# Gated linear attention on one core: gate ranks transposed with the keys a tile ahead, half of a compact score copy on another engine, weight splits tied to another instruction

## The chip, the core and the metric

The kernel runs on one NeuronCore of a Trainium2 chip. The metric is the device time of one execution in microseconds; the profile is one execution taken by the hardware profiler on the same core. The engines are TensorE (PE: matrix products and transposes; PEld is its load of the stationary operand), ScalarE (ACT: activations and copies), VectorE (DVE), GpSimd (POOL) and SyncE (SP), which here only issues DMAs. Products land in PSUM, in eight banks; everything else lies in SBUF.

## The reference

One step of a decoder layer for 2048 prompt tokens and 64 sample tokens, all float32. What matters here is group B of the mixer, gated linear attention with 4 heads (key width 64, value width 128):

```python
h = rms_norm(x, g_mix_pre)
proj = jnp.einsum('btd,de->bte', h, w_in)      # ... gq, gk, gv, gr and the 16 gate ranks glr
log_a = jax.nn.log_sigmoid(einsum('btr,rk->btk', glr, w_gk2) + b_gk) / GLA_GATE_TEMP
b = jnp.cumsum(log_a, in a chunk)              # decay of the keys
k_rel = jnp.exp(where(causal, b_t - b_s, -inf)) * k_s
o_intra = einsum(einsum(q, k_rel), v)          # inside a chunk
o_inter = (q * exp(b)) @ S                     # from the state
S = exp(b_last) * S + (k * exp(b_last - b)).T @ v
o = rms_norm(o, g_gla) * silu(gr)
```

Around it stand the combined input projection, sliding-window attention (group A), the output projection with norms and residual, and a squared-ReLU MLP of width 4096.

## The kernel before

The work is in tiles of 128 tokens: 16 of the prompt (`NB`) and one of the sample (number `NB`). The stages follow each other on the chip: projection and attention of group A (to about 345 us), the gated linear attention with its own projections (to about 745 us), the output projection, and the MLP, whose weights and activations are multiplied by a scheme of seven products on split operands. Float32 operands are split into a high and a low part and multiplied three times (`hi*hi`, `hi*lo`, `lo*hi`).

**The order of the work.** TensorE's order is the order of the code (the helper `te`, class `InOrder` at line 120, chains every product to the one before it). For ScalarE, VectorE, GpSimd and SyncE in this stage there is no such chain: a planner sorts their instructions at compile time, by the order of the code and by its own estimate of when each is ready, and may issue a later tile's step before an earlier tile's. `tc.issue_after(ins)` ties what a block adds on the engine of `ins` to come after `ins`.

**The gated linear attention.** `gla(i)` (line 1067) is a generator for tile i. It yields numbers: at each `yield n`, the driver (lines 1346 to 1356) takes n products from `fill` and puts them on TensorE; half way it advances `side`, the steps of the sample tile, once. `fill` (`products`, line 1293) are the projections of later tiles (tile name `gproj`, 24 products of 128x384 for each of four chunks of weights), then, when the last tile is projected, the first output projections (`out`), whose weights `wo` are loaded into the place of the chunks that are done. `G_FILL` (line 65) holds the five fills of a tile.

In a tile, in the order of the code:
- `qk_T` (964) turns queries and keys (`gqk`, bank d); VectorE copies the keys to `kt`, ScalarE the queries to `qz`.
- After the first fill (34), `finish_out` of the tile before ends: `ogT`, the transposed output.
- `decays` of the next tile (933), up to line 940: for an even tile the gate ranks of two tiles are turned (`pg`, bank d) and copied by ScalarE to `glrT`. Then the second fill (6).
- `put_diagonal` (1023): the diagonal of the scores into the compact tile `AH`.
- `level_sums` and `weighted` for seven levels (block sizes 1 to 64): running sums of the logs in `before` and `after`, their exponentials in `dec`, and keys and queries weighted with them, `XK` and `XQ`. Each level needs the one before it, in turn on VectorE (1014, 1015) and ScalarE (1011, 1013).
- `keys_decayed` (995): the keys decayed to the end of the tile, `kdT`.
- The rest of `decays` of the next tile: `z`, two products with `glrT`, then three ScalarE steps (945 to 947) and one VectorE step (948) that gives the next tile's `before`.
- `gate` (950), the swish gate `sg`. Then the third fill (24).
- `kdT` turned (bank e) and copied by ScalarE to `kd`. Then the fourth fill (8).
- The scores by level: `gl` and `gh` (bank c, 1101 to 1109), and `ds` (bank d), what the tile adds to the state.
- VectorE places the scores with masks in `AH` (1021, six levels). ScalarE copies the largest level from `gh` (1122) and then the two halves of `AH` (1124, 64 partitions x 256 each) to `AT`. VectorE makes the new state `S` (1127). Then the fifth fill (20).
- `o` (bank e): for each head the query part with the old state and `AT` with the values.
- A step of `split_wo` (1256): one of eight raw tiles of the output weights is split into a high part (ScalarE, 218) and a low part (VectorE, 219), stored to DRAM, and a further raw tile is loaded. The block stands under `tc.issue_after(done.ins)`, `done` being the second state update on VectorE.

`before`, `after`, `dec`, `sg`, `qz`, `AH` and `AT` have one place each, `kt`, `kd` and `zt` two. Banks d and e have one place, the other kinds (a, b, c) two. The sample tile goes through the same helpers from `gla_sample` (1153), with bank b.

Of the kernel before, what the change touches and what calls it, by code (L numbers as in the profile page):

```python
# [15 lines left out]
AF = mybir.ActivationFunctionType  # L16
# [5 lines left out]
P = 128  # L22
# [3 lines left out]
NB = T // P  # L26
# [35 lines left out]
G_FIRST = (0, 1)  # L62
G_NEXT = (NB, *range(2, NB))
G_ORDER = (0, 1, 2, 3)
G_FILL = (34, 6, 24, 8, 20)
S_WAIT = (3, 6)
WO_PARTS = ((), (0, 1, 2), (3, 4, 5), (6, 7))
B_ORDER = (*(j + b for j in range(4) for b in (0, 4)), NB, *(j + b for j in range(4) for b in (8, 12)))
# [47 lines left out]
def f32(ap):  # L116
    return ap.bitcast(F32)
# [23 lines left out]
def hybrid_step_kernel(ctx: ExitStack, tc: tile.TileContext, I, O):  # L141
    nc = tc.nc
# [20 lines left out]
    te, ac, dv = (InOrder(tc, engine) for engine in (nc.tensor, nc.scalar, nc.vector))  # L163
# [4 lines left out]
    def bank(shape, kind, name):  # L168

        return ps.tile(shape, F32, tag=kind, name=name, bufs=1 if kind in "de" else 2)  # L170
# [21 lines left out]
    ident = cpool.tile([P, P], F32, name="ident")  # L192
# [77 lines left out]
    glr = gp_pool.tile([P, (NTILE + 1) // 2, 2, HD], F32R, name="glr")  # L270
# [133 lines left out]
    half_of = slice(HD), slice(HD, P)  # L404
# [479 lines left out]
    def places(name, shape, n=1, kind=F32):  # L884
        return cycle([sp.tile(shape, kind, name=f"{name}{u}") for u in range(n)])

    S = [sp.tile([P, 2, P], F32, name=f"S{u}") for u in range(2)]
    glrT = [sp.tile([P, P], F32R, name=f"glrT{u}") for u in range(3)]
    AT = sp.tile([P, 4, P], F32, name="AT")
    AH = sp.tile([P, 4, HD], F32, name="AH")  # L890
# [10 lines left out]
    zts, kdTs = places("zt", [P, 2, P], 2), places("kdT", [P, 2, P])  # L901
# [28 lines left out]
    for t in (s_xk, s_qz, s_at, s_after):  # L930
        nc.gpsimd.memset(t, 0.0)

    def decays(i, n, before, kind="d"):

        gt = glrT[i // 2 % 2 if i < NB else 2]
        if i % 2 == 0:
            pg = bank([P, P], kind, f"pg_{i}")
            te.transpose(pg, f32(glr[:, i // 2]).rearrange("p a r -> p (a r)"), ident)
            nc.scalar.activation(gt, pg, AF.Copy)
        yield  # L940
        z = bank([P, 2, n], kind, f"z_{i}")
        for g in range(2):
            te.matmul(z[:, g], wgk[:, i % 2, g * P : (g + 1) * P], gt[:, :n], start=True, stop=True)
        t = next(zts)[:, :, :n]
        nc.scalar.activation(t, z, AF.Abs)
        nc.scalar.activation(t, t, AF.Exp, scale=-1.0)
        nc.scalar.activation(t, t, AF.Ln, bias=1.0)
        nc.vector.scalar_tensor_tensor(before, z, 0.0, t, op0=ALU.min, op1=ALU.subtract)
# [15 lines left out]
    def qk_T(i, gp, n, kind="d"):  # L964

        pt = bank([P, 2, 2, n], kind, f"gqk_{i}")
        for g in range(2):
            for a in range(2):
                src = gp[:n, (1 - a) * 256 + g * P : (1 - a) * 256 + (g + 1) * P]
                te.transpose(pt[:, g, a, :], src, ident[:n, :n])  # L970
        kt, q = (next(kts), qz) if n == P else (s_kt, s_qz)
        nc.vector.tensor_copy(kt, pt[:, :, 0, :])
        for r, rr in enumerate(half_of):
            nc.scalar.activation(q[rr, r], pt[rr, :, 1, :], AF.Copy, scale=0.125)
        return kt
# [16 lines left out]
        out = xq[:, l].rearrange("p r g (m b) -> p r (g m) b", b=b)  # L992
        nc.vector.tensor_tensor(out, dr.unsqueeze(1).to_broadcast(list(out.shape)), pairs(q, b, 1), op=ALU.mult)

    def keys_decayed(after, kt, kdT, n, kind, kd):

        nc.scalar.activation(kdT, after, AF.Exp, scale=1.0 / 16)
        nc.vector.tensor_tensor(kdT, kdT, kt, op=ALU.mult)
        yield
        pk = bank([P, 2, P], kind, f"kdT_{n}")  # L1000
        for g in range(2):
            te.transpose(pk[:n, g, :], kdT[:, g, :], ident)
        nc.scalar.activation(kd[:n], pk[:n].rearrange("p g k -> p (g k)"), AF.Copy)

    def level_sums(before, after, dec, l, b):

# [10 lines left out]
    def put_level(at, gm, mk, b):  # L1017

        dst = halves(at, b)[1]
        m = mk.rearrange("p (m b) -> p m b", b=b).unsqueeze(1).to_broadcast(list(dst.shape))  # L1020
        nc.vector.copy_predicated(dst, m, gm.rearrange("p h (m b) -> p h m b", b=b))

    def put_diagonal(i, at, gp, n):

        pr = next(prs)
        nc.vector.scalar_tensor_tensor(pr[:n], gp[:n, 0:256], 0.125, gp[:n, 256:512], op0=ALU.mult, op1=ALU.mult)
        dg = sp.tile([P, 4], F32, tag="dg", name=f"dg_{i}", bufs=2)
        nc.vector.tensor_reduce(dg[:n], pr[:n].rearrange("p (h d) -> p h d", h=4), op=ALU.add, axis=AX.X)
        shape = [n, 4, HD]
        nc.vector.copy_predicated(at, dmsk[:n].unsqueeze(1).to_broadcast(shape), dg[:n].unsqueeze(2).to_broadcast(shape))  # L1030
# [29 lines left out]
    def decayed(i):  # L1060

        before, after = next(befores), next(afters)
        yield from decays(i, P, before)
        nc.gpsimd.memset(after, 0.0)
        pre[i] = before, after

    def gla(i, gp, og=iter(())):

        assert {(i, 0), (i, 1)} <= projected
        before, after = pre.pop(i)
        next(og, None)
        kt = qk_T(i, gp, P)
        dec = next(decs)
        following = decayed(i + 1) if i < NB - 1 else iter(())
        yield G_FILL[0] if i else 24, True
        deque(og, 0)
        next(following, None)
        yield G_FILL[1], True  # L1080
        put_diagonal(i, AH, gp, P)
        for l, b in enumerate(LEVELS):
            level_sums(before, after, dec, l, b)
            if l == NL - 1:
                kd = next(kds)
                turned = keys_decayed(after, kt, next(kdTs), P, "e", kd)
                nc.scalar.activation(dec[:, NL], before, AF.Exp, scale=1.0 / 16)
            weighted(XK, XQ, dec, kt, qz, l, b)
        next(turned)
        deque(following, 0)  # L1090
        assert {(i, c) for c in range(4)} <= projected
        sg = gate(i, gp, P)
        yield G_FILL[2], True
        deque(turned, 0)
        yield G_FILL[3], True
        low = bank([P, 4, 4, P // 4], "c", f"gl_{i}")
        high = bank([P, 512], "c", f"gh_{i}")
        mid = high[:, :256].rearrange("p (l h q) -> p l h q", l=2, h=4)
        far = high[:, 256:384].rearrange("p (r q) -> p r q", r=2)
        levels = [*(low[:, l] for l in range(4)), *(mid[:, l] for l in range(2))]  # L1100
        for l, gm in enumerate(levels):
            for g in range(2):
                keys = XK[:, l, g] if l else kt[:, g]
                for u, uu in enumerate(half_of):
                    te.matmul(
                        gm[uu, 2 * g : 2 * g + 2], keys[:, uu], XQ[:, l, :, g, u * 32 : u * 32 + 32], start=True, stop=True
                    )
        for g in range(2):
            te.matmul(far[half_of[g]], XK[:, NL - 1, g, :HD], XQ[:, NL - 1, :, g], start=True, stop=True)
        gv = gp[:, 512:1024]  # L1110
        ds = bank([P, 2, P], "d", f"ds_{i}")
        for h in range(4):
            te.matmul(
                ds[half_of[h % 2], h // 2], kd[:, h * HD : (h + 1) * HD], gv[:, h * P : (h + 1) * P],
                start=True, stop=True,
            )
        qd = next(qds)
        nc.vector.tensor_tensor(qd, qz, dec[:, NL].unsqueeze(1).to_broadcast([P, 2, 2, P]), op=ALU.mult)
        for l, gm in enumerate(levels):
            put_level(AH, gm, msk[:, l], LEVELS[l])  # L1120
        for g in range(2):
            nc.scalar.activation(AT[:HD, 2 * g : 2 * g + 2, HD:], far[half_of[g]], AF.Copy)
        for uu in half_of:
            nc.scalar.activation(AT[uu, :, uu], AH[uu], AF.Copy)
        So, Sn = S[i % 2], S[(i + 1) % 2]
        for g in range(2):
            done = nc.vector.scalar_tensor_tensor(
                Sn[:, g], So[:, g], dec[:, NL, g, P - 1 : P], ds[:, g], op0=ALU.mult, op1=ALU.add
            )
        yield G_FILL[4], True  # L1130
        o_ = bank([P, 4, P], "e", f"o_{i}")
        for h in range(4):
            if i > 0:
                te.matmul(o_[:, h, :], qd[:, h % 2, h // 2], So[:, h // 2], start=True, stop=False)
            te.matmul(o_[:, h, :], AT[:, h, :], gv[:, h * P : (h + 1) * P], start=i == 0, stop=True)
        with tc.issue_after(done.ins):
            next(wo_parts, None)
        ogs_of[i] = og = finish_out(i, lambda h: o_[:, h, :], sg, P, "e")
        if i == NB - 1:
            yield from og  # L1140
            for g in range(2):
                for r in range(2):
                    nc.sync.dma_start(O["gla_prompt"][0, 0, 2 * g + r], Sn[half_of[r], g])
# [944 lines left out]
```

## Time and profile before

| what | value |
|---|---|
| median of 3 runs | 2264.04 us (2259.86 to 2265.18) |
| the profiled execution | 2263.19 us, span 2261.4 us |
| instructions | 34140 |
| granted TensorE clock, mean | 0.995 of full speed |
| TensorE / VectorE / ScalarE / GpSimd busy | 97 / 68 / 54 / 11% |
| gated linear attention | about 345 to 745 us |

How to read the profile: L12 is line 12 of the kernel; `out<-in` are the program's names of the tiles written and read; a row of the waits says who waited for whom, with the total in us, how often, and the longest; a row of a timeline gives start, duration, engine, line and operation, and in brackets the idle time of the engine before it with what ended it. Several instructions of one kind in a row are merged (x4). The granted clock is a share of full speed. Ends of products are modelled, so two products in a row can overlap in the timeline.

### The profile page before, as it was taken

The page shows a single profiled execution, that of the slowest core. Times are in us where ns is not written, and L with a number is a line of the kernel's source. Part 1 is how long each engine was busy: PE and PEld are TensorE (multiplying, and loading weights), DVE is VectorE, ACT ScalarE, POOL GpSimd, SP SyncE. Part 2 cuts the span into 40 slices and gives each one's busy share as a digit, 9 for nine tenths or more (in the row PEclk, how much of TensorE's full clock was granted, in tenths as well). Part 3 has the DMA queues.
Part 4 walks back from the last instruction along what each step waited for, and adds up shares of the span by engine and source line. Part 5 has one row for each costly group of instructions (what it writes and reads, how often), then busy time and mean ns, then how long its engine had stood idle before and what let it go on. Part 6 is the DMA issues. An engine that isn't in the chain of part 4 may idle for free.

```text
span 2261.4 us, 34140 instructions
## 1 busy us (share of the span) xinstructions
PE 2183.5 (97%) x11816; PEld 1868.7 (83%) x11816; DVE 1529.9 (68%) x3102; ACT 1221.4 (54%) x2594; POOL 259.4 (11%) x417
## 2 busy tenths in 40 slices
PE   8999999999999999999999999999999999999998
PEld 7888888999998887788888788887888888788876
DVE  5888877776765565777788664447676666455566
ACT  5778766556664444555545564334544454454444
POOL 3566422111111110000000000000000000000000
PEclk9999999999999999999999999999999999999999
DMA  6334322214335558967777885557644443766675
GB/s 231 119 133 143 102 90 82 67 57 148 126 122 196 184 181 312 313 222 243 251 254 253 284 290 181 180 167 231 195 179 154 154 154 140 252 201 198 192 241 169
DMA packets 237256, 417.81 MB, mean 185 GB/s; under 512 B 25172, under 2 KB 137276, under 8 KB 232972
## 3 DMA queue, kind: packets, MB, share of 16 engines
q1 hardware_dynamic: 237084, 415.64, 54.8%
q8 instruction: 93, 1.52, 0.3%
q14 instruction: 79, 0.65, 0.1%
HBM read 268.44 MB, written 148.18 MB: 184 GB/s over the span
## 4 chain that ended last, share of the span: by engine, by line
PE 64%; DVE 15%; ACT 8%; DMA 8%; issue 3%; POOL 1%; SPq 0%; DVEq 0%; ACTq 0%; POOLq 0%
PE dn L130 21%; PE uc L130 6%; PE ua L130 6%; PE out L1250 6%; PE gproj L130 5%; PE ud L130 3%; PE ue L130 3%; PE ub L130 3%; DMA rt<-t_d 3%; DVE s L130 2%; PE proj L130 2%; PE dsam L130 1%; DVE pl L130 1%; PE o L130 1%; PE sam L130 1%
## 5 line engine op out<-in xcount | busy, mean ns | idle before, releaser
L130 PE MATMUL dn<-o0t,o0s 128*128 128x512 f32 x896 | 350.7, 391 | 9.0 <-ACT o0t L218 8.8
L130 PE MATMUL dn<-o1t,o0s 128*128 128x512 f32 x896 | 351.3, 392 | 3.1 <-DVE o1t L219 3.1
L130 PE MATMUL dn<-o0t,o1s 128*128 128x512 f32 x896 | 349.9, 391 | 0.0
L219 DVE TENSOR_TENSOR o1s<-rs,o0s 128x512 fp32r<-128x512 f32 x224 | 154.6, 691 | 197.2 <-ACT o0s L218 182.8
L218 ACT ACTIVATE o0s<-rs 128x512 fp32r<-128x512 f32 x224 | 141.1, 630 | 249.9 <-PE dn L130 206.0
L130 PE MATMUL gproj<-wg,gx 128*128 128x384 f32 x1408 | 268.5, 343 | 0.1
L130 PEld LDWEIGHTS gproj<-wg,gx 128*128 128x128 f32 x1408 | 241.6, 189 | 4.5 <-issue 4.3
L130 ACT ACTIVATE st<-st 128x512 f32<-128x512 f32 x224 | 141.1, 630 | 158.9 <-DVE st L130 154.9
L130 PEld LDWEIGHTS dn<-o0t,o0s 128*128 128x128 f32 x896 | 168.6, 188 | 48.9 <-ACT o0t L218 11.9
L130 PEld LDWEIGHTS dn<-o1t,o0s 128*128 128x128 f32 x896 | 168.5, 188 | 43.7 <-DVE o1t L219 7.9
L130 PEld LDWEIGHTS dn<-o0t,o1s 128*128 128x128 f32 x896 | 168.5, 188 | 35.0
L219 DVE TENSOR_TENSOR o1t<-rt,o0t 128x512 fp32r<-128x512 f32 x224 | 153.9, 687 | 64.3 <-ACT o0t L218 63.9
L218 ACT ACTIVATE o0t<-rt 128x512 fp32r<-128x512 f32 x224 | 139.6, 624 | 91.7 <-DMA rt<-t_d 70.0
L130 PE MATMUL uc<-H,s 128*128 128x512 f32 x768 | 186.7, 391 | 0.0
L130 PE MATMUL ua<-H,w 128*128 128x512 f32 x744 | 179.2, 390 | 0.0
L130 PEld LDWEIGHTS uc<-H,s 128*128 128x128 f32 x768 | 144.1, 188 | 31.9
L130 PEld LDWEIGHTS ua<-H,w 128*128 128x128 f32 x744 | 138.7, 188 | 28.2
L1250 PE MATMUL out<-wo,mt 128*128 128x512 f32 x680 | 158.9, 392 | 1.9 <-ACT mt L218 1.8
L1250 PEld LDWEIGHTS out<-wo,mt 128*128 128x128 f32 x680 | 126.5, 188 | 28.6 <-ACT mt L218 2.1
L208 POOL TENSOR_TENSOR frs<-rs_v,half 128x1 f32<-128x1 f32 (+1 forms) x13 | 8.4, 657 | 1230.2 <-DVE rs_v L206 1230.2
L130 DVE TENSOR_TENSOR st<-st 128x512 f32<-128x512 f32 x160 | 110.7, 692 | 35.1 <-ACT st L130 31.8
L130 ACT ACTIVATE s<-t 128x1024 fp32r<-128x1024 f32 x62 | 65.8, 1061 | 93.5 <-PE ud L130 29.0
(388 smaller groups left out, 4231.2 us busy)
## 6 DMA issues: line engine op xcount, KB each, us to landing
s_d<-st SPq DMA_DIRECT2D x32, 1792.0 KB, 7.6
rs<-s_d SPq DMA_DIRECT2D x224, 256.0 KB, 2.9
raw<-in_w_up SPq DMA_DIRECT2D x64, 512.0 KB, 5.2
rt<-t_d SPq DMA_DIRECT2D x128, 256.0 KB, 3.3
rt<-in_w_down SPq DMA_DIRECT2D x96, 256.0 KB, 2.8
t<-in_w_down SPq DMA_DIRECT2D x64, 256.0 KB, 3.7
t_d<-t SPq DMA_DIRECT2D x32, 512.0 KB, 6.6
gx<-xt_d SPq DMA_DIRECT2D x28, 512.0 KB, 4.8
```

The source lines that it names most:

```text
L130: ins = call(*a, **k)
L208: nc.gpsimd.tensor_tensor(out, v[:n], e, op=ALU.pow)
L218: nc.scalar.activation(hi, src, AF.Copy)
L219: vector.tensor_tensor(lo, src, f32(hi), op=ALU.subtract)
L1250: te.matmul(banks[c], x, w[:, c * 512 : (c + 1) * 512], start=k + u == 0, stop=k == KT - 1 and u == len(products) - 1,)
```

## The change

Three edits in the gated linear attention.

1. The gate ranks of tiles i+2 and i+3 are turned in `keys_decayed` of an even tile i, into a third part of the bank that takes `kdT`, and copied from there to `glrT` behind `kd`. Only tile 0 and the sample tile still turn theirs in `decays`. `decays` no longer yields between that and `z` for other tiles, so that `z` of the next tile comes right behind the first fill; the second fill stands behind `z` and the level sums, and is 14, the third 16. Tile 0's `decays` takes its banks from kind b.
2. The half of `AH` on partitions 64 to 127 is copied to `AT` by VectorE, the other half by ScalarE as before.
3. `done`, behind which the split of the output weights is tied, is ScalarE's copy of that half in place of VectorE's state update.

```diff
@@ -62,7 +62,7 @@
 G_FIRST = (0, 1)
 G_NEXT = (NB, *range(2, NB))
 G_ORDER = (0, 1, 2, 3)
-G_FILL = (34, 6, 24, 8, 20)
+G_FILL = (34, 14, 16, 8, 20)
 S_WAIT = (3, 6)
 WO_PARTS = ((), (0, 1, 2), (3, 4, 5), (6, 7))
 B_ORDER = (*(j + b for j in range(4) for b in (0, 4)), NB, *(j + b for j in range(4) for b in (8, 12)))
@@ -930,14 +930,17 @@
     for t in (s_xk, s_qz, s_at, s_after):
         nc.gpsimd.memset(t, 0.0)
 
+    def ranks_T(pair, out):
+        te.transpose(out, f32(glr[:, pair]).rearrange("p a r -> p (a r)"), ident)
+        return out
+
     def decays(i, n, before, kind="d"):
 
         gt = glrT[i // 2 % 2 if i < NB else 2]
-        if i % 2 == 0:
+        if i in (0, NB):
             pg = bank([P, P], kind, f"pg_{i}")
-            te.transpose(pg, f32(glr[:, i // 2]).rearrange("p a r -> p (a r)"), ident)
-            nc.scalar.activation(gt, pg, AF.Copy)
-        yield
+            nc.scalar.activation(gt, ranks_T(i // 2, pg), AF.Copy)
+            yield
         z = bank([P, 2, n], kind, f"z_{i}")
         for g in range(2):
             te.matmul(z[:, g], wgk[:, i % 2, g * P : (g + 1) * P], gt[:, :n], start=True, stop=True)
@@ -992,15 +995,18 @@
         out = xq[:, l].rearrange("p r g (m b) -> p r (g m) b", b=b)
         nc.vector.tensor_tensor(out, dr.unsqueeze(1).to_broadcast(list(out.shape)), pairs(q, b, 1), op=ALU.mult)
 
-    def keys_decayed(after, kt, kdT, n, kind, kd):
+    def keys_decayed(after, kt, kdT, n, kind, kd, pair=0):
 
         nc.scalar.activation(kdT, after, AF.Exp, scale=1.0 / 16)
         nc.vector.tensor_tensor(kdT, kdT, kt, op=ALU.mult)
         yield
-        pk = bank([P, 2, P], kind, f"kdT_{n}")
+        pk = bank([P, 3, P], kind, f"kdT_{n}")
         for g in range(2):
             te.transpose(pk[:n, g, :], kdT[:, g, :], ident)
-        nc.scalar.activation(kd[:n], pk[:n].rearrange("p g k -> p (g k)"), AF.Copy)
+        ranks = ranks_T(pair, pk[:, 2]) if pair else None
+        nc.scalar.activation(kd[:n], pk[:n, :2].rearrange("p g k -> p (g k)"), AF.Copy)
+        if pair:
+            nc.scalar.activation(glrT[pair % 2], ranks, AF.Copy)
 
     def level_sums(before, after, dec, l, b):
 
@@ -1060,7 +1066,7 @@
     def decayed(i):
 
         before, after = next(befores), next(afters)
-        yield from decays(i, P, before)
+        yield from decays(i, P, before, "d" if i else "b")
         nc.gpsimd.memset(after, 0.0)
         pre[i] = before, after
 
@@ -1076,18 +1082,18 @@
         following = decayed(i + 1) if i < NB - 1 else iter(())
         yield G_FILL[0] if i else 24, True
         deque(og, 0)
-        next(following, None)
-        yield G_FILL[1], True
         put_diagonal(i, AH, gp, P)
         for l, b in enumerate(LEVELS):
             level_sums(before, after, dec, l, b)
             if l == NL - 1:
                 kd = next(kds)
-                turned = keys_decayed(after, kt, next(kdTs), P, "e", kd)
+                pair = i // 2 + 1 if i % 2 == 0 and i < NB - 2 else 0
+                turned = keys_decayed(after, kt, next(kdTs), P, "e", kd, pair)
                 nc.scalar.activation(dec[:, NL], before, AF.Exp, scale=1.0 / 16)
             weighted(XK, XQ, dec, kt, qz, l, b)
         next(turned)
         deque(following, 0)
+        yield G_FILL[1], True
         assert {(i, c) for c in range(4)} <= projected
         sg = gate(i, gp, P)
         yield G_FILL[2], True
@@ -1120,11 +1126,11 @@
             put_level(AH, gm, msk[:, l], LEVELS[l])
         for g in range(2):
             nc.scalar.activation(AT[:HD, 2 * g : 2 * g + 2, HD:], far[half_of[g]], AF.Copy)
-        for uu in half_of:
-            nc.scalar.activation(AT[uu, :, uu], AH[uu], AF.Copy)
+        nc.vector.tensor_copy(AT[half_of[1], :, half_of[1]], AH[half_of[1]])
+        done = nc.scalar.activation(AT[half_of[0], :, half_of[0]], AH[half_of[0]], AF.Copy)
         So, Sn = S[i % 2], S[(i + 1) % 2]
         for g in range(2):
-            done = nc.vector.scalar_tensor_tensor(
+            nc.vector.scalar_tensor_tensor(
                 Sn[:, g], So[:, g], dec[:, NL, g, P - 1 : P], ds[:, g], op0=ALU.mult, op1=ALU.add
             )
         yield G_FILL[4], True
```

## The prediction

> **What bounds the kernel now.** I read the page first (busy time by engine), then the busy time by stretch, then who waited for whom on TensorE inside the stage that the change touches, then its timelines engine by engine.
>
> ```profile
> PE 2183.5 (97%) x11816; PEld 1868.7 (83%) x11816; DVE 1529.9 (68%) x3102; ACT 1221.4 (54%) x2594; POOL 259.4 (11%) x417
> ```
>
> TensorE is busy for 97% of the span; only what shortens its own waits, or the time that it runs slow, can shorten the kernel. The gated linear attention runs from 345 to 750 us. The sum of eight stretches there, and TensorE's waits there:
>
> ```profile
> sum 405.00, PE 385.28 PEld 361.46 DVE 277.03 ACT 250.08 POOL 70.45; mean PE 48.16 PEld 45.18 DVE 34.63 ACT 31.26 POOL 8.81
> ```
>
> ```profile
> PE o L130 <- ACT AT L1124: 11.0, 10, 2.2
> PE gqk L130 <- DVE before L948: 3.0, 1, 3.0
> PE z L130 <- ACT glrT L939: 3.0, 4, 0.9
> PE out L130 <- DMA wo<-wo_d: 1.4, 5, 0.5
> PE ogT L130 <- DVE og L1042: 0.8, 1, 0.8
> PE ds L130 <- ACT kd L1003: 0.4, 1, 0.4
> ```
>
> TensorE is idle for 405.0 - 385.3 = 19.7 us, and the six rows name 19.6 of it. Rows one, two and three, 17.0 us, are the waits that the diff edits. Three of them in TensorE's timeline (start, duration, what, and in brackets the idle time before it):
>
> ```profile
> 355.46 1.11 PE L130 MATMUL gqk<-ident,gp 128*128 128x128 f32 x4 [3.01 <-DVE before L948]
> ...
> 570.38 0.49 PE L130 MATMUL o<-gp,AT 128*128 128x128 f32 x2 [1.74 <-ACT AT L1124]
> ...
> 708.94 0.49 PE L130 MATMUL o<-gp,AT 128*128 128x128 f32 x2 [2.15 <-ACT AT L1124]
> ```
>
> The longest two cost more than their idle time. Columns: stretch, its length, busy times, then granted clock, DMA share and GB/s.
>
> ```profile
> 352.00:356.00 4.00, 0.99 (x7) 0.85 (x6) 1.97 (x4) 2.45 (x6) 3.29 (x7) 0.86 0.75 244
> 356.00:360.00 4.00, 4.00 (x19) 4.00 (x18) 3.67 (x13) 2.86 (x9) 0.47 (x1) 0.71 0.00 0
> ...
> 708.00:712.00 4.00, 3.06 (x19) 3.06 (x19) 0.45 (x1) 1.75 (x7) 0.00 (x0) 0.74 0.85 321
> 712.00:716.00 4.00, 4.00 (x22) 4.00 (x21) 3.03 (x13) 2.13 (x9) 1.01 (x1) 0.84 0.43 140
> ```
>
> Behind the 3.01 us wait the clock is short by 4 x 0.14 + 4 x 0.29 = 1.7 us of full speed; behind the 2.15 us wait by 4 x 0.26 + 4 x 0.16 = 1.7 us. Here each wait of over 2 us was followed by such a loss.
>
> **Why the o products wait.** One ordinary tile, engine by engine.
>
> ```profile
> 602.00 1.29 PE L130 MATMUL gproj<-wg,gx 128*128 128x384 f32 x6
> 603.13 0.33 PE L130 MATMUL z<-glrT,wgk 128*128 128x128 f32 x2
> ...
> 616.10 0.49 PE L130 MATMUL o<-gp,AT 128*128 128x128 f32 x2 [0.71 <-ACT AT L1124]
> ```
>
> ```profile
> 595.50 0.28 ACT L1037 ACTIVATE ojunk<-o 128x128 bf16<-128x128 f32 x1 [1.92 <-PE o L130]
> ...
> 598.22 1.05 ACT L218 ACTIVATE wop<-wor 128x1024 fp32r<-128x1024 f32 x1
> ...
> 614.76 0.55 ACT L1122 ACTIVATE AT<-gh 64x128 f32<-64x128 f32 x2 [1.40 <-DVE AH L1021]
> 615.22 0.83 ACT L1124 ACTIVATE AT<-AH 64x256 f32<-64x256 f32 x2
> ```
>
> ```profile
> 595.94 0.42 DVE L972 COPY kt<-gqk 128x256 f32<-128x256 f32 x1 [1.87 <-PE gqk L130]
> 596.40 0.90 DVE L991 TENSOR_TENSOR XK<-dec,kt 128x128 f32<-128x128 f32 x4
> ...
> 605.27 0.42 DVE L948 SCALAR_TENSOR_TENSOR before<-z,zt 128x256 f32<-128x256 f32 x1 [1.75 <-ACT zt L947]
> ...
> 612.23 1.58 DVE L1021 COPY_PREDICATED AH<-c,gl 128x128 f32<-128x128 uint8 x4
> ```
>
> The reader is to see one chain. z is issued at 603.13; three ScalarE steps later VectorE forms the next tile's logs (605.27), runs that tile's level sums, and only at 612.23 places this tile's scores in AH; ScalarE begins to copy at 614.76 and ends at about 616.05, 0.71 us after TensorE wanted AT. VectorE stood idle for 1.75 us before 605.27: the chain is late because z is.
>
> **The change, part by part** (lines of the kernel before).
>
> *z earlier* (L65, L1079-1080, L936-940). The rank transpose and its copy leave the place in front of z, and the first short fill goes behind z. z comes 6 products earlier, 603.13 - 602.00 = 1.13 us, and the four waits for glrT go: 3.0 us off TensorE. The transpose itself stays, with kdT and a tile ahead, so TensorE's work is the same; bank e holds a third more, and o in that bank comes 8 + 20 fill products later, which hide the moved ScalarE copy. No DMA moves. The level chain starts about 1.1 us sooner, and more where z had waited: the idle 1.75 us takes it up. The side steps of the sample group keep their number and shift by a few fills; no row of TensorE's waits names them, so I cost them at nothing (against: their inputs share VectorE, at most a few tenths each).
>
> *Half of AT on VectorE* (L1123-1124). ScalarE's two copies take 0.83 us together; one remains, so AT is ready 0.41 us sooner if VectorE's copy fits beside it. The trace has no such copy. Its rows bound it: 0.90/4 = 0.22 us for half the elements, 0.42 us for as many out of PSUM. I take 0.3 us, nearer the second row by size; beside ScalarE's 0.46 + 0.41 us of far and near copies it is hidden at either end. Behind it on VectorE wait the next diagonal and kt; before kt lie 1.87 us idle.
> [...]
>
> *Weight splits behind it* (L1127, L1136). Now the VectorE half of a split is tied behind the state update and can stand in front of the last placing of scores:
>
> ```profile
> 567.52 1.22 DVE L219 TENSOR_TENSOR wop<-wor,wop 128x1024 fp32r<-128x1024 f32 x1
> 568.66 0.29 DVE L1021 COPY_PREDICATED AH<-c,gh 128x128 f32<-128x128 uint8 x1
> ```
>
> That is 568.66 - 567.52 = 1.14 us of the 1.74 us wait at 570.38. Afterwards the ScalarE half (1.05 us) is tied behind AT's ScalarE copy, in a gap that lasts 1.92 us before ojunk, and VectorE's half must follow it, so it can't precede AH. Behind the ScalarE half waits ojunk, hidden by 0.9 us. The next raw load and the two stores on SP's queue come some 3 us later; the stored weights are read only after the last projection.
>
> So the chain gains 1.1 us (z) + 0.41 us (AT), and 1.1 us more where a split stood in the way. Against the nine o waits before the last, 11.0 - 2.15 = 8.85 us in all and none over 1.74, I take **8.5 us** off; **3.0 us** for z.
>
> *The last long wait* (708.94). Here splits of the mix tile, tied to nothing in the diff, stand in front of the scores:
>
> ```profile
> 703.89 1.22 DVE L219 TENSOR_TENSOR mt<-mt 128x1024 fp32r<-128x1024 f32 x1
> ```
>
> They stay. The scores end at 705.1 + 2.5 us (612.23 to 614.76), less 0.8 us if the sums that now run between them are done, so 706.8; with 0.46 + 0.41 us AT is ready at 707.6, against TensorE at 706.8. The wait falls from 2.15 to 0.8 us, and without a wait over 2 us the clock holds: 1.4 + 1.7 = **3.1 us**.
>
> *The start* (L1063: tile 0's gate scores in bank b). gqk no longer waits for bank d: it can start at 355.46 - 3.01 = 352.45, and 54 fill products follow (6 in 1.13 us above, so at most 10.2 us). But kdT of tile 0 needs the whole level chain, which does not begin sooner:
>
> ```profile
> 364.80 0.42 DVE L998 TENSOR_TENSOR kdT<-kdT,kt 128x256 f32<-128x256 f32 x1
> ```
>
> ```profile
> 366.85 0.38 PE L130 MATMUL kdT<-ident,kdT 128*128 128x128 f32 x2
> ```
>
> TensorE is there at about 363 and waits for 365.2, or 364.8 as kt is early: a new wait of some 2 us takes the place of the 3.0. kdT then starts 1.7 to 2.0 us sooner than 366.85, less up to 1.7 if the clock drops again. I take **1.0 us**.
>
> Sum: 8.5 + 3.0 + 3.1 + 1.0 = 15.6 us. The profiled execution took 2263.19 us (span 2261.4), 0.85 below the median of 2264.04; 2263.2 - 15.6 + 0.85 gives **2248.5 us**.
>
> **The rivals.**
>
> *Only the copy counts.* ScalarE's and VectorE's orders are the planner's. If VectorE's sums start no sooner, each o wait loses 0.41 us, two lose 1.1 more: about 5.2 of the 8.85; the last wait falls to 1.74 us, which at 570 us did not lower the clock (2.1 us in all); with 3.0 and 1.0, 11.3 us: 2252.7. For: the chain is long. Against: the idle 1.75 us.
>
> *The transfers take it back.* The next bound after the stage is the load of the output weights (1.4 us of waits). If these loads came no sooner, the whole 15.6 us would return as a longer wait for wo: 2264, no change. For: DMA share 0.85 at 708. Against: 0.43 just after, and the loads wait for the last projection to free their place, so they move with TensorE.
>
> *Slower: VectorE's copy queued late.* The planner could put it behind a whole weight split and the state updates, 1.22 + 0.5 + 0.3 = 2.0 us after AH, in the eight tiles with splits and in the last. AT is now ready 0.46 + 0.83 = 1.3 us after AH, so it would come 0.7 us later; beyond 4/9 = 0.4 us later this eats the 4 us that z and the start bring. In the five tiles that wait longest the wait would then be about 2 us or more and cost the clock as well: 9 x 0.7 + 5 x 1.7 - 4 = +10.8 us, 2275. Against: a split now follows ScalarE's copy, which is done no earlier than 0.87 us after AH.
>
> *No clock recovery.* If the idle time is not what lowers the clock, 1.7 us less is won: 2250.2. The 0.71 and 0.74 that follow just these two waits speak against it.
> [...]
>
> **How the numbers follow.** Forecast 0.62 (2244 to 2252; the low end is a start with no new wait and nothing left at the last o); no clock recovery 0.08; only the copy 0.13; transfers 0.10; slower 0.07. The range 2243 to 2261 leaves out the last two and takes in the bounds of every term. What a measurement can tell from no change is 0.3%, 6.8 us: faster 0.79, same 0.14, slower 0.07.
>
> **What would show it.** Right: the rows for glrT and gqk gone from TensorE's waits, o's row under 2 us in total, L948 starting over a microsecond sooner behind ogT, no L219 row between two L1021 rows of a tile, a kdT wait of about 2 us near 362. Wrong: o's row still above 5 us, new rows for ogT or kdT in ordinary tiles, or a longer row for wo<-wo_d.

## The result and the profile after

The changed kernel took 2251.77 us (median of 4 runs, 2249.57 to 2252.46) beside 2262.93 us for the kernel before on the same chip (4 runs): a ratio of 0.9953, 95% interval 0.9941 to 0.9965, or 11 us less. Measured once more beside the last experiments it took 2254.03 us (5 runs) against 2262.70: 0.9960, 0.9948 to 0.9972. The forecast was 2248.5 us; the sign and about seven tenths of the 15.6 us came, but only part of it from the steps that the forecast gave. By its own list of signs (the o row still above 5 us) its mechanism was wrong in part.

The profiled execution took 2249.57 us (span 2247.8). First the same eight stretches from 345 to 750 us of the changed kernel, busy time by engine:

```profile
sum 405.00, PE 390.92 PEld 366.39 DVE 290.56 ACT 245.24 POOL 71.77; mean PE 48.86 PEld 45.80 DVE 36.32 ACT 30.65 POOL 8.97
```

Then TensorE's waits in the changed kernel from 330 to 745 us (total, times, longest):

```profile
PE o L130 <- ACT AT L1130: 7.9, 10, 1.9
PE gproj L130 <- ACT dec L1017: 1.8, 1, 1.8
PE gproj L130 <- DVE gp_s L213: 1.1, 1, 1.1
PE ogT L130 <- DVE og L1048: 1.1, 1, 1.1
PE out L130 <- DMA wo<-wo_d: 0.9, 3, 0.4
```

TensorE is now idle for 405.0 - 390.9 = 14.1 us of the stage instead of 19.7. The rows for z and gqk are gone. But the o row, forecast at under 2 us, is 7.9, and still counts ten waits. The granted clock is 1.00 throughout the stage, where before it was short by 3.4 us.

Why o still waits is seen in one ordinary tile of the changed kernel: TensorE's timeline, then ScalarE's, then VectorE's (start, duration, what, and in brackets the idle time before it).

```profile
595.02 0.60 PE L130 MATMUL ogT<-ident,og 128*128 128x128 f32 x4
595.37 0.42 PE L130 MATMUL z<-glrT,wgk 128*128 128x128 f32 x2
...
609.31 0.49 PE L130 MATMUL o<-gp,AT 128*128 128x128 f32 x2 [0.44 <-ACT AT L1130]
```

```profile
596.20 0.63 ACT L961 ACTIVATE sg<-sg 128x512 f32<-128x512 f32 x1 [0.64 <-DVE sg L960]
596.74 0.58 ACT L1063 ACTIVATE mo<-ogT 128x512 f32<-128x512 f32 x1
597.22 0.38 ACT L948 ACTIVATE zt<-z 128x256 f32<-128x256 f32 x1
...
608.39 0.56 ACT L1128 ACTIVATE AT<-gh 64x128 f32<-64x128 f32 x2 [1.55 <-DVE AH L1027]
608.86 0.40 ACT L1130 ACTIVATE AT<-AH 64x256 f32<-64x256 f32 x1
609.16 1.04 ACT L218 ACTIVATE wop<-wor 128x1024 fp32r<-128x1024 f32 x1
```

```profile
598.52 0.42 DVE L951 SCALAR_TENSOR_TENSOR before<-z,zt 128x256 f32<-128x256 f32 x1 [1.76 <-ACT zt L950]
598.98 0.81 DVE L1020 TENSOR_TENSOR after<-after,before 128x128 f32<-128x128 f32 x1
...
608.40 0.29 DVE L1129 COPY AT<-AH 64x256 f32<-64x256 f32 x1
```

z starts 0.35 us behind ogT and is done at 595.37 + 0.42 = 595.79 us, and nothing comes of it. Its first step on ScalarE (zt, L948) stands at 597.22 behind the gate's last Exp (L961, which itself waits 0.64 us for VectorE) and the copy of ogT (L1063). The logs (L951) come 598.52 - 595.02 = 3.50 us behind ogT and VectorE still idles 1.76 us in front of them; in the tile of the kernel before that the forecast read, the same distance was 3.62 us. So in this tile the chain gained 0.12 us, not 1.1. In the ordinary tiles whose z had waited the logs did come clearly sooner: 3.51 us behind ogT instead of 4.30 (ogT at 617 us here, 624 before), 3.50 instead of 4.75 (662 and 669). The lower rows are the part that worked: VectorE's half of AT takes 0.29 us beside ScalarE's copies, and the split (L218) stands behind AT.

### The profile page after: what moved, and what is told of

Same layout as the page of the kernel before. It is cut to its first block, busy times and chain, and to the rows that moved or that the text cites. A ratio compares the mean times of both kernels' runs of the same rounds, so it can differ in the third digit from the quotient of the medians.

```text
span 2247.8 us, 34153 instructions
## 1 busy us (share of the span) xinstructions
PE 2182.2 (97%) x11816; PEld 1870.2 (83%) x11816; DVE 1539.4 (68%) x3118; ACT 1214.0 (54%) x2578; POOL 259.6 (12%) x417
## 4 chain that ended last, share of the span: by engine, by line
PE 51%; DMA 4%; DVE 2%; ACT 1%; issue 1%; POOL 0%; SPq 0%; DVEq 0%; ACTq 0%; POOLq 0%
PE dn L130 23%; PE uc L130 7%; PE ua L130 7%; PE ud L130 4%; PE ue L130 4%; PE ub L130 4%; DMA rt<-t_d 3%; PE sam L130 1%; PE dsam L130 1%; DMA rs<-s_d 1%; DMA H<-hp_d 1%; DVE o1t L219 0%; ACT o0t L218 0%; DMA t<-in_w_down 0%; DMA bx<-in_x_prompt 0%
## 5 line engine op out<-in xcount | busy, mean ns | idle before, releaser
L218 ACT ACTIVATE o0s<-rs 128x512 fp32r<-128x512 f32 x224 | 141.1, 630 | 259.1 <-PE dn L130 211.4
L218 ACT ACTIVATE o0t<-rt 128x512 fp32r<-128x512 f32 x224 | 139.6, 624 | 83.9 <-DMA rt<-t_d 63.0
```

What stands on the lines that cost most here:

```text
L218: nc.scalar.activation(hi, src, AF.Copy)
```

## The experiments

Two theories at the start. **A**, the forecast: z earlier starts the chain sooner and cures the o waits, the copy helps, the splits get out of the way. **B**, the rival "only the copy counts". Twelve kernels ran, each against the kernel before on the same chip.

### The four edits, one at a time

*Ranks a tile ahead*, alone: the parts of the diff in `ranks_T`, `decays`, `keys_decayed`, `decayed` and `gla`, with

```diff
-G_FILL = (34, 6, 24, 8, 20)
+G_FILL = (34, 14, 16, 8, 20)
```

> Only the first edit on the kernel before: ranks a tile ahead, z behind the first fill, fills of 14 and 16, tile 0's logs in bank b; both halves of AT stay on ScalarE and the split stays tied to the state update. Theory A (the record's: an earlier z starts the next tile's level sums about 1.1 us sooner, so the scores are placed sooner): z's waits 3.0 us gone and the o waits down from 11.0 to about 3 us; 9 to 12 us faster. Theory B (z's three ScalarE steps stand behind the gate and the output copy in ScalarE's queue, so the sums start no sooner): z's waits gone, o waits still 9 to 12 us, the last one over 2 us with the clock loss behind it; 4 to 6 us faster.

Measured: 2261.92 us, ratio 1.0001 (0.9993 to 1.0010). The z and gqk rows are gone, and the o row went up, from 11.0 to 12.6 us. Neither theory's figure came: an edit that takes two rows off TensorE was worth nothing. This kernel holds the bank b edit too, which alone is worth 2.7 us (below), so what is left of it lost about as much; its profile has three stretches at half speed in the stage where the kernel before has two.

*Half of AT on VectorE*, alone:

```diff
-        for uu in half_of:
-            nc.scalar.activation(AT[uu, :, uu], AH[uu], AF.Copy)
+        nc.vector.tensor_copy(AT[half_of[1], :, half_of[1]], AH[half_of[1]])
+        nc.scalar.activation(AT[half_of[0], :, half_of[0]], AH[half_of[0]], AF.Copy)
```

> Only the second edit on the kernel before: the upper half of AH goes to AT by VectorE. Both theories: each o wait is shorter by 0.41 us, 11.0 to about 7 us; the last one falls to about 1.74 us, and if waits over 2 us are what lowers the clock, the granted clock behind it stays at 1.00: 3.9 + 1.7 = 5.6 us faster; without the clock 3.9. z and gqk waits as before (3.0 and 3.0).

Measured: 2260.07 us, 0.9995 (0.9985 to 1.0005): the expected 3.9 to 5.6 us did not come. The o waits, in three rows, are 4.8 + 3.3 + 1.5 = 9.6 us, not 7. VectorE's timeline in this kernel, then TensorE's:

```profile
374.88 1.32 DVE L1123 COPY AT<-AH 64x256 f32<-64x256 f32 x1
...
595.76 1.22 DVE L219 TENSOR_TENSOR wop<-wor,wop 128x1024 fp32r<-128x1024 f32 x1
597.01 0.29 DVE L1123 COPY AT<-AH 64x256 f32<-64x256 f32 x1
```

```profile
597.45 0.46 PE L130 MATMUL o<-gp,AT 128*128 128x128 f32 x2 [1.67 <-DVE AT L1123]
```

The forecast's rival on the slower side is here at work: where a tile has a split, VectorE's copy is queued behind it, and o waits 1.67 us for 0.29 us of work. In tile 0 the copy met one of GpSimd's products for the sample's gate (1.27 us from 374.77) and took 1.32 us; o then waited 0.80 us. No term of the forecast's sum counts such a meeting.

*Splits behind AT*, alone (`done` is ScalarE's second copy of AT instead of the state update):

> Only the third edit on the kernel before: the split of the output weights tied behind ScalarE's second AT copy, both halves on ScalarE. Both theories: no VectorE row of a split between two placings of scores; the two o waits that had one (1.42 and 1.74 us) lose about 1.1 us each, the others stay: 11.0 to about 8.8 us, 2 us faster, hardly to be told from no change by time. If a tied split costs something elsewhere (ojunk, kt), new rows for ogT or kdT appear.

Measured: 2258.94 us, 0.9993 (0.9984 to 1.0002); o row 9.3 us in 8 waits, z 2.9, gqk 3.1. Of the two o waits that had a split between their scores, the one at 523 us (1.42 us) is gone and the one at 570 us went from 1.74 to 1.02; of the others, the one at 661 us grew from 0.81 to 1.47.

*Tile 0's gate scores in bank b*, alone (one line, `"d" if i else "b"`):

> Only tile 0's logs in bank b on the kernel before. Theory of the record: the gqk wait of 3.0 us goes, TensorE waits some 2 us later in tile 0 instead, no clock loss or another one: 0 to 2 us faster. Rival: the new waits add up to the old one (2.9 us), none is over 2 us, and only the 1.7 us of lost clock come back: 1.8 us faster; granted clock 1.00 from 352 to 360 us.

Measured: 2258.39 us, 0.9988 (0.9979 to 0.9996), 2.7 us less. The 3.0 us gqk wait is gone with its clock loss; gproj waits 1.3 us and kdT 1.0 us instead.

### The changed kernel less one edit

Singly the edits give 0, 1, 2 and 3 us (the first of these with bank b in it), together 11. So the ranks, the copy and the tie were each taken out of the changed kernel. By now a third theory stood, the **loop**: in ordinary tiles the pace is set by o, its squares, og, the gate (whose single place waits for og), ScalarE's queue, the logs, the level sums, the placing of scores, AT and the next o. By this theory the z waits were off that loop, and taking them away moves the same idle time to o.

*Without the ranks* (the copy, the tie and bank b stay):

> The changed kernel without its rank edit (the copy on VectorE, the splits behind it and bank b stay; the ranks and z stay where they were). Loop theory: in ordinary tiles the next tile's logs start when ScalarE comes free behind the gate and the copy of ogT, not when z is done, so z's place is worth little: within 2.5 us of the changed kernel's 2251.8, that is 2250 to 2254.5, with the z row back at 3 us and the o row lower than the changed kernel's 7.9 us by about as much. Rival (the sum of the prediction): without the rank edit the 3.0 us of z waits and 1.1 us in each o wait that is left come back, 3.0 + 4 = 7 us: 2259.

Measured: 2251.82 us, 0.9956 (0.9944 to 0.9968), the time of the changed kernel. Its TensorE waits:

```profile
PE o L130 <- ACT AT L1124: 5.0, 7, 1.7
PE z L130 <- ACT glrT L939: 2.9, 4, 0.8
```

5.0 + 2.9 = 7.9 us, the o row of the changed kernel: as totals, the rank edit moves 2.9 us of waiting from z to o. Wait by wait it is two things that cancel. The o products of tiles 1 and 5, first in this kernel, then in the changed one:

```profile
399.25 0.49 PE L130 MATMUL o<-gp,AT 128*128 128x128 f32 x2 [0.28 <-ACT AT L1124]
...
498.92 0.49 PE L130 MATMUL o<-gp,AT 128*128 128x128 f32 x2 [0.47 <-ACT AT L1124]
```

```profile
396.98 0.49 PE L130 MATMUL o<-gp,AT 128*128 128x128 f32 x2 [1.62 <-ACT AT L1130]
...
498.10 0.49 PE L130 MATMUL o<-gp,AT 128*128 128x128 f32 x2 [1.90 <-ACT AT L1130]
```

These two waits grew by 1.34 + 1.43 = 2.8 us, nearly the whole growth of the row. In the ordinary tiles behind them (520 to 690 us) three z waits of 0.76 us each are gone and the o waits are what they were, 2.5 us here and 2.7 in the changed kernel; seven tiles, from the o of tile 7 to that of tile 14, take 155.5 us in the changed kernel (in both of its profiles) and 157.3 here. From the o of tile 0 to that of tile 7 it is the other way round, 169.8 and 167.6 us. So, against the loop theory, the z waits of the ordinary tiles did come off, and the tiles that share VectorE and ScalarE with the sample group gave the gain back. VectorE's timeline of the changed kernel in tile 5 shows how:

```profile
492.61 0.16 DVE L206 TENSOR_SCALAR rs_v<-ossq 64x4 f32<-64x4 f32 x1 [1.53 <-ACT ojunk L1043]
493.89 1.12 DVE L1048 SCALAR_TENSOR_TENSOR gp_s<-s_ob,ors,s_sg 64x128 f32<-64x128 f32 x4 [1.11 <-POOL ors L208]
494.93 0.43 DVE L1027 COPY_PREDICATED AH<-c,gl 128x128 f32<-128x128 uint8 x1
```

All placings of the tile's scores (L1027) stand behind the sample's gp_s, which starts 13.45 us behind ogT (480.44), and VectorE idles 1.53 + 1.11 us in front of it. In this kernel gp_s starts 12.46 us behind ogT and one of the placings stands ahead of it. Whether the new place of the ranks or the new fills of 14 and 16 shift these steps is open, and so is the cause in tile 1.

*Without VectorE's copy* (both halves on ScalarE):

> The changed kernel with both halves of AT on ScalarE again (ranks, splits behind AT and bank b stay). Theory: AT comes 0.41 us later in each of the ten tiles that wait, and in those just short of waiting: o row 7.9 + 4 to 5 = 12 to 13 us, time 2251.8 + 4 to 5 = 2256 to 2257. Rival (the advance of z is what counts, the copy is hidden): 2252 to 2253.

Measured: 2261.88 us, 0.9998 (0.9989 to 1.0007). The whole gain is gone, twice the 4 to 5 us that the theory gave. TensorE's row in this kernel:

```profile
PE o L130 <- ACT AT L1130: 12.4, 10, 2.2
```

The waits grew by 12.4 - 7.9 = 4.5 us, as expected. The rest goes with the clock: this profile has four stretches of 3.41 us at half speed in the stage, 1.7 us each, 6.8 us, where the changed kernel's has none (see below). Two of them stand behind o waits that are longer without the copy (2.05 us at 401 us, 2.15 at 711). One stands behind the gproj wait of 1.82 us, which the changed kernel has too, and one behind the sample's small products named at the end. So 4.5 + 3.4 us can be put down to the copy; the other 3.4 us of this profile are a matter of where the stretches fell.

*Without the tie* (`done` is the state update again):

> The changed kernel with the weight splits tied behind the state update again (ranks, VectorE's copy and bank b stay). Theory: in the tiles with splits VectorE's half of a split (1.22 us) stands between the scores and VectorE's half of AT, as in the run of the copy alone; o row 12 to 14 us, with bank b's gain left: 2258 to 2261. Rival (each edit is worth its own): only the 1.14 us of two tiles comes back: 2254.

Measured: 2258.18 us, 0.9978 (0.9969 to 0.9987): 4 us over the 2254.03 that the changed kernel took when it was measured beside it. TensorE's o rows are

```profile
PE o L130 <- DVE AT L1129: 5.6, 6, 1.2
PE o L130 <- ACT AT L1130: 5.3, 3, 1.9
PE o L130 <- ACT gp L613: 2.0, 2, 1.2
```

12.9 us. The first and the third row, 7.6 us in eight waits, are VectorE's copy queued behind a split; the third names a ScalarE step, but in both of its tiles the copy (at 545.46 and 637.09 us), behind a split, is what ends last in front of o. Copy and tie are one edit: each alone is within 2 us of nothing, and taking either away costs 4 us or more.

### Cutting the loop

*Logs ahead of the gate's last Exp* in ScalarE's order, on top of the changed kernel:

```diff
+        logs = logs_of.get(i + 1) if n == P and i + 1 < NB else None
+        with tc.issue_after(logs.ins) if logs else nullcontext():
-        nc.scalar.activation(t[:n], t[:n], AF.Exp)
+            nc.scalar.activation(t[:n], t[:n], AF.Exp)
```

> The changed kernel with one more order: the gate's last Exp on ScalarE is tied behind the Ln of the next tile's logs. Loop theory: the logs start 0.6 us sooner than behind that Exp (0.63 us), plus the 0.6 us in which ScalarE waited for the gate's VectorE step: about 1.0 to 1.2 us sooner behind ogT than now (3.5 us falls to about 2.4). The o waits of the ordinary tiles 6 to 13 (0.24 to 0.61 us, 2.7 us together) go; those behind a split or at the sample's end stay. Time 2251.8 - 2.7 = 2249. Rival 1: VectorE's queue, not ScalarE's, holds the sums: the logs start sooner but the o waits stay at 7.9 us and the time at 2252. Rival 2: the later gate delays og: a new ogT row, up to 0.6 us in ten tiles, 2252 to 2258.

Measured: 2260.47 us, 0.9999 (0.9991 to 1.0008); the gain is gone. VectorE's timeline of this kernel, then GpSimd's (POOL), in a tile whose ogT starts at 603.17:

```profile
605.62 0.42 DVE L953 SCALAR_TENSOR_TENSOR before<-z,zt 128x256 f32<-128x256 f32 x1 [0.69 <-ACT zt L952]
606.08 0.29 DVE L1024 TENSOR_TENSOR after<-after,before 128x128 f32<-128x128 f32 x1
606.47 1.22 DVE L1025 TENSOR_TENSOR before<-before 128x128 f32<-128x128 f32 x1
607.79 1.27 DVE L1024 TENSOR_TENSOR after<-after,before 128x128 f32<-128x128 f32 x1
```

```profile
606.25 1.29 POOL L966 TENSOR_TENSOR sg<-sg,gp 128x512 f32<-128x512 f32 x1 [6.23 <-ACT sg L965]
607.62 1.29 POOL L968 TENSOR_TENSOR sg<-sg,ggla 128x512 f32<-128x512 f32 x1
```

The logs do start 605.62 - 603.17 = 2.45 us behind ogT instead of 3.50. But the gate's two GpSimd products now fall among the level sums, and the two sums that meet them take 1.22 and 1.27 us instead of 0.29 and end just behind them: 1.9 us lost for 1.05 won. In the tile of the changed kernel shown above the first product had run in VectorE's idle time, and only the 0.81 us sum at 598.98 met the second. ScalarE's copy of kd, queued behind the exponentials of those sums, came late too (a new ds row, 3.0 us in 8 waits), and in tile 0 gproj waited 4.2 us. In the changed kernel's trace all 17 sums that began while a product of GpSimd ran ended 0.15 to 0.25 us behind it, after 0.32 to 1.27 us; the 206 that met none took 0.27 to 0.32. Not every VectorE step was held up so: ten steps of XQ (128x256) that began in such a product ended within it, after 0.42 to 0.45 us, and those that met none took 0.41 to 0.42. None of the 16 copies of AT in that kernel, 0.29 us each, met a product. The kernel before had such sums too (one of 0.82 us, L1014 at 605.72, right behind the logs that the forecast read).

*Two places for the gate* (`places("sg", [P, 512], 2)`), so that it need not wait for og:

> The changed kernel with two places for the gate instead of one, so that the gate need not wait until og has read the last one. Loop theory: ScalarE does the gate while it waits for o, and only the copy of ogT stands in front of the logs: these start about 0.9 to 1.2 us sooner behind ogT; o waits of the ordinary tiles (2.7 us together) go: 2249 to 2250. Rival: the gate's four steps (2.5 us) stand in front of the squares of o instead, og comes later, a new ogT row of up to 0.6 us in ten tiles: 2252 to 2258, o row unchanged.

Measured: 2256.81 us, 0.9968 (0.9956 to 0.9981). The o row fell to 5.4 us, but og came later: the ogT row rose from one wait of 1.1 us to 3.9 us in 4 waits, which is the rival's mechanism, in three further tiles rather than ten. From 577 us on the logs start 3.2 to 4.2 us behind ogT as in the changed kernel, so there the loop was not cut. Twice (397.88 and 423.21 us) VectorE's copy of AT met a gate product of GpSimd and took 1.03 and 1.02 us.

*The gate's two products on VectorE* (`engine = nc.vector if n == P else nc.gpsimd`, used for both), on top of the changed kernel. In the tile of that kernel shown above VectorE idles 1.76 us in front of the logs, and the sum that met GpSimd's second product takes 0.81 us instead of 0.29:

> The changed kernel with the gate's two products of the prompt tiles on VectorE instead of GpSimd. [...]

Measured: 2249.81 us, 0.9940 (0.9927 to 0.9953). VectorE's timeline in this kernel, behind an ogT at 596.66, and TensorE's waits:

```profile
598.51 0.69 DVE L963 TENSOR_TENSOR sg<-sg,gp 128x512 f32<-128x512 f32 x1
599.23 0.69 DVE L965 TENSOR_TENSOR sg<-sg,ggla 128x512 f32<-128x512 f32 x1
600.17 0.42 DVE L951 SCALAR_TENSOR_TENSOR before<-z,zt 128x256 f32<-128x256 f32 x1 [0.24 <-ACT zt L950]
600.63 0.29 DVE L1021 TENSOR_TENSOR after<-after,before 128x128 f32<-128x128 f32 x1
```

```profile
PE o L130 <- ACT AT L1131: 4.3, 3, 1.6
```

The products fill VectorE's idle time, the first sum is 0.29 us again, and all seven waits of the ordinary tiles are gone; the three that are left stand behind steps of the sample group (tiles 1 and 5) and behind the mix tile's splits. This kernel lies 4 us below the changed one measured beside it, though the intervals overlap (up to 0.9953, and from 0.9948).

*The same without the ranks:*

> The same two products on VectorE, but in the kernel without the rank edit (run before: 2251.8 us, o row 5.0 us, z row 2.9 us). Theory: o row about 3 us, z row still 2.9, time 2249 to 2250, equal to the one with the rank edit within 1.5 us. Rival: with the o waits gone the z waits are what is left, and the rank edit is then worth its 3 us: this one 3 us longer than the one with the rank edit.

Measured: 2249.31 us, 0.9945 (0.9932 to 0.9959); o row 2.8 + 0.7, z row 3.0. Equal to the one with the rank edit within the noise: taken whole, it is worth nothing here either.

### Where the clock goes down

*The changed kernel again*, for a second profile:

> The changed kernel itself once more, for a second profile. Theory (half speed is given in stretches of 3.41 us that lie on a fixed grid, behind a stretch in which TensorE was idle for more than about half): the same waits return within 0.3 us, but the places of the slow stretches shift as a whole, since the run starts elsewhere on the grid: up to three of the four waits of 1.6 to 1.9 us in the stage may be followed by one now, each 1.7 us. Rival (only waits of over 2 us lower the clock): none in the stage again. Time 2250 to 2253 by both.

Measured: 2254.03 us, 0.9960. The o row came back (8.1 us, ten waits), and so did the gproj wait of 1.82 us. Stretches of 3.41 us of this second profile around that wait (length, busy times, then granted clock, DMA share, GB/s):

```profile
364.65:368.06 3.41, 1.59 (x10) 1.43 (x10) 3.41 (x11) 3.00 (x8) 0.31 (x1) 1.00 0.45 153
368.06:371.48 3.42, 3.42 (x44) 2.98 (x43) 1.75 (x7) 2.77 (x10) 0.00 (x0) 0.50 0.01 4
371.48:374.89 3.41, 3.41 (x41) 3.24 (x40) 3.31 (x15) 1.63 (x6) 0.00 (x0) 1.00 0.00 0
```

and of the first profile of the same kernel around the same wait:

```profile
360.22:363.63 3.41, 1.73 (x10) 1.41 (x9) 3.41 (x14) 2.88 (x10) 0.31 (x1) 1.00 0.14 38
363.63:367.05 3.42, 3.28 (x47) 3.02 (x49) 3.32 (x11) 3.33 (x10) 0.00 (x0) 1.00 0.36 117
```

One wait, once followed by half speed and once not. In the 14 profiles of this study every slow stretch has a granted clock of 0.50, lasts 3.41 us or twice that (but at the very end of the run), and within a profile they lie whole multiples of 3.413 us apart (in the first profile of the changed kernel the one at 32.53 us and the next, at 889.28, lie 251 times that apart). The first 12 to 16 us, for which a profile has no clock record, and the end of the run are left out of what follows. On that grid, all 48 stretches at full speed in which TensorE was idle for over 1.9 us were followed by half speed. Of the stretches at full speed with less than 1.54 us of idle time only four were, those named at the end; between 1.54 and 1.9 us it went either way. So in these profiles a wait of some 1.6 to 2.2 us cost 1.7 us more or not, as the grid fell: in the kernel with the rank edit alone a 2.07 us wait lay within one stretch and half speed followed, while its 2.15 us wait at 709 us was cut in two by the grid, with 1.38 us idle in one stretch and 0.77 in the next, and none did.

Idle time and slow stretches (1.7 us each) of the stage from 345 to 750 us, in each kernel's profile, account for the measured times within about 4 us:

| kernel | idle, us | slow stretches | sum against before | time against before (from the ratio) |
|---|---|---|---|---|
| before | 19.7 | 2 | | |
| ranks only | 17.7 | 3 | -0.3 | +0.2 |
| copy only | 18.9 | 4 | +2.6 | -1.1 |
| tie only | 17.7 | 2 | -2.0 | -1.6 |
| bank b only | 17.9 | 1 | -3.5 | -2.7 |
| changed | 14.1 | 0 | -9.0 | -10.6 |
| changed, again | 13.4 | 1 | -8.0 | -9.1 |
| without ranks | 12.1 | 0 | -11.0 | -10.0 |
| without copy | 17.9 | 4 | +1.6 | -0.5 |
| without tie | 17.7 | 0 | -5.4 | -5.0 |
| logs first | 16.3 | 2 | -3.4 | -0.2 |
| two gates | 15.3 | 0 | -7.8 | -7.2 |
| products on VectorE | 11.9 | 1 | -9.5 | -13.6 |
| the same, no ranks | 11.5 | 0 | -11.6 | -12.4 |

(Sum: idle time less 19.7, plus 1.7 us for each slow stretch over two.) A profile's stretches are one draw of the grid, a median is taken over several, which can be part of what is left. Taken directly, the time from the first gproj product to the last ogT fell from 454.7 us before to 444.1 in the changed kernel's first profile: 10.6 of the 13.6 us between the two spans.

## Why the prediction was right, and where it was wrong

- **What bounds the kernel**: right. TensorE's idle time and its clock in this stage give the difference within about 4 us in every kernel of the table.
- **The sum**: the forecast's number came partly by luck. In the first profile the nine o waits before the last fell from 8.85 to 6.2 us, 2.7 us where 8.5 were forecast: this is the term that was mis-sized. z gave its 3.0 us, the last wait 0.4 + 1.7 of 3.1, and the start 0.1 of idle time and 1.7 of clock, where 1.0 in all was forecast.
- **z earlier, 3.0 us and a chain 1.1 us sooner**: this step failed. "The idle 1.75 us takes it up" took the start of the logs for a question of z; in the tile shown ScalarE's queue (the gate's Exp, the copy of ogT) held them, 3.50 us behind ogT against 3.62. The edit as a whole was worth nothing: with and without it the kernel takes 2251.8 us. In the ordinary tiles the z waits did come off (1.8 us in seven tiles).
- **The side steps of the sample group, "I cost them at nothing"**: this term was not nothing. With the rank edit the o waits of tiles 1 and 5, where the sample's steps stand among those of the tile, are 2.8 us longer than without it, and that takes back what the ordinary tiles gained.
- **Half of AT on VectorE, 0.41 us a tile**: right in mechanism. 0.29 us against the 0.3 estimated, hidden in the changed kernel, and 4.5 us of waits come back without it. Undersized, since two of these waits, near 2 us, also cost clock; the whole gain goes when it is taken out, part of it by where the slow stretches fell. A meeting with GpSimd, which no term counts, did not come in the changed kernel, but did three times in two others (1.02 to 1.32 us).
- **Splits behind AT**: right, and more than the 1.14 us in two tiles. Without the tie the copy itself stands behind the split, which is the slower rival's mechanism; the tie is the condition for the copy. Together these two explain most of the fall of the o row from 11.0 to 5.0 us in the kernel without the ranks: ten waits less up to 0.41 us and two less a split, the working of "only the copy counts". That its 11.3 us lie by the 11.2 measured is luck in part: it counts 3.0 us for z, which the time did not keep, and its 5.2 us for nine waits come to 5.6 from the waits of the trace before.
- **The last long wait, 2.15 to 0.8 us**: 1.73 us, since two splits of the mix tile still stand in front of the scores and the sums still run between them. VectorE's timeline of the changed kernel, and TensorE's:

```profile
692.62 1.23 DVE L219 TENSOR_TENSOR mt<-mt 128x1024 fp32r<-128x1024 f32 x1 [0.53 <-ACT mt L218]
...
694.55 1.21 DVE L219 TENSOR_TENSOR mt<-mt 128x1024 fp32r<-128x1024 f32 x1
```

```profile
699.18 0.49 PE L130 MATMUL o<-gp,AT 128*128 128x128 f32 x2 [1.73 <-ACT AT L1130]
```

  So 0.4 us of the 1.4 came, and the 1.7 us of clock.
- **The start, 1.0 us**: the wait of some 2 us came, as gproj's 1.82 us, with 1.1 us beside it; bank b alone is worth 2.7 us, since the 3.0 us wait's clock loss goes with it. Its new wait cost the clock in the second profile of the changed kernel and not in the first.
- **Transfers take it back**: no. The wo row is 0.9 us in the first profile and 1.4, as before, in the second. **No clock recovery**: the clock did recover in the stage, but no bound of 2 us on a wait decided it: gproj's 1.82 us was followed by half speed in one profile of the changed kernel and not in the other. The forecast's 3.4 us was a draw, not a sum that each run pays.

What stays open: how much idle time a stretch needs between 1.54 and 1.9 us, what in the rank edit shifts the sample's steps, and why the logs-first kernel lies 3 us above its row of the table.

## What to carry to other kernels

Taking a wait away from the bounding engine is worth nothing if the idle time comes back at another of its waits: take the edit out of the changed kernel, and see, wait by wait and not only by the totals, where the idle time goes. Before an operation is called early, read the queue of the engine that does its next step. And before a step is put in an idle place on VectorE, look at what GpSimd does there: with the logs first, two sums beside its products took 1.22 and 1.27 us instead of 0.29.

## What the hardware showed unexpectedly

Half speed also followed a stretch in which TensorE was never idle. In the kernel with the rank edit alone, two stretches on the grid and the products that fill the end of the first:

```profile
415.34:418.75 3.41, 3.41 (x29) 3.10 (x27) 2.22 (x8) 2.89 (x11) 0.11 (x1) 1.00 0.00 0
418.75:422.16 3.41, 3.41 (x34) 2.97 (x35) 1.43 (x2) 0.69 (x2) 0.20 (x1) 0.50 0.35 86
```

```profile
416.12 1.10 PE L130 MATMUL s_oi<-s_at,gp_s 64*128 64x64 f32 x8
417.16 2.17 PE L130 MATMUL s_oe<-s_qz,s 128*128 128x16 f32 x16
```

The sample's eight products of 64 columns and sixteen of 16 columns fill the time, but the clock went down behind them as behind idle time. In four of the 14 profiles 2.6 us or more of this block (2.60 to 2.88) fell into one stretch of the grid, and half speed followed each time with no idle time in the stretch; where 2.2 us or less fell into one stretch, in all the others, it never did. A VectorE addition of 128x128 fp32 took 0.29 us where it met no GpSimd product and up to 1.31 us beside one (L1015 at 373.85 us in the kernel before). A copy of 64x256 fp32 from SBUF to SBUF took 0.29 us on VectorE and 0.40 us on ScalarE in the changed kernel, and up to 1.32 us on VectorE beside a GpSimd product in the kernel with the copy alone.
